# Product-key routing of an expert layer: unnormed stream transposed, the norm's factor moved into the gates, single fp32 query products, and the later heads' routing tied step by step behind the dot products

## The chip, the cores and the metric

The kernel runs on one core of one Trainium2 chip. The metric is the device time in microseconds (us) of one launch. TensorE is called PE here, VectorE DVE, ScalarE ACT, GpSimd POOL, and SyncE SP, which only starts transfers.

## The reference

Two transformer blocks run one after the other on 256 tokens of width 1024. The change touches the second half of the first block, a feed-forward layer with product keys (8 heads, 16384 experts), in float32:

```python
h = h + peer_ffn(rms_norm(h, norm_ffn), peer_w_query, peer_sub_keys, peer_down, peer_up)

q = (xf @ w_query).reshape(T, 8, 2, 128)
s = einsum('thcd,hckd->thck', q, sub_keys)            # two tables of 128 keys per head
top_s, top_i = top_k(s, 16)                           # best 16 of each table
cand_s = top_s[:, :, 0, :, None] + top_s[:, :, 1, None, :]
cand_i = top_i[..., 0, :, None] * 128 + top_i[..., 1, None, :]
best_s, pos = top_k(cand_s, 16)                       # best 16 sums: 16 experts per head and token
gates = softmax(best_s)
# per token, over its 128 chosen experts e:
a = gelu(dot(x, expert_down[e]))                      # exact gelu
out = sum(gate_e * a_e * expert_up[e])
```

`rms_norm(x, g)` is x times 1/sqrt(mean(x^2) + 1e-6), one factor for each token, times the gain g for each column.

## The kernel before

`emit` runs the phases in order. Phase A (`phase_a`) is the first block's mixer; its last step adds the output projection into the stream `x` (L589, two tiles of 128 tokens `tt`, two halves of 512 columns). Phase B (`phase_b`) is the layer above. Phases C and later are the second block.

At the start of phase B, `rms_norm` (L233 to L244) turns the sums of squares into one factor r for each token (POOL's pow, L240) and writes `xn` = x r on DVE (L244). `transpose_split` transposes `xn` on PE (L254) into `XH`, the rounded part (ACT, L258), and `XL`, the rest (DVE, L263). POOL multiplies `xn` by the gain row into `xg` (L716), which the dot products use.

`peer_route` is one head's routing, a Python generator that yields after each step. It loads 1 MB of query weights (`qraw`, L613, four buffers, SP's queue), and makes the query product `q` as three products of rounded parts: `part` splits each 512 columns of weights into `hi` (ACT, L291) and `lo` (DVE, L295), and PE runs hi XH, lo XH and hi XL (L306 to L308, for the first head L332 to L338): 48 matmuls of 256 columns for a head. Then come the copy `qT` (ACT, L619), four score matmuls `s` (L625), and on DVE the two rounds of top 16 (L602 to L606), index arithmetic (L653 to L675) and the expert numbers `idx` (L678). The gates take an Exp on ACT (L682).

The main loop has 128 rounds k (8 heads of 16 experts). In each, `fetch` gathers one row of 8 KB (down and up weights together) for each of 256 tokens: two indirect transfers of 1 MB, issued by POOL (L728) into one of ten buffers `gb`, four rounds ahead. `products` makes the two dot products on DVE (L735, `dots`) and the gelu on ACT (L737). `sums`, for the round before, multiplies by the gate (DVE, L740), makes a diagonal matrix `dg` for each token tile (ACT, L743) and adds the up rows with four fp32 matmuls of 512 columns into four PSUM tiles `u` (PE, L745). A buffer is free for the next gather when its matmuls in L745 are done. When the query weights' four buffers come free, SP loads phase C's first weights into them (`wt`, L820 and L822, four of 1 MB, the first in halves).

Head 0's routing runs to its end before the loop. Head h's is written into the rounds of head h-1, two steps in each of the first eleven rounds and the rest in the twelfth. That is only the order in which the program is written: a scheduler puts each engine's instructions in an order of its own, and each engine then runs its list in that order and waits at the front of it.

Of the kernel before, what the change touches and what calls it, by code (L numbers as in the profile page):

```python
# [9 lines left out]
F32 = mybir.dt.float32  # L10
# [175 lines left out]
class Kern:  # L186
# [25 lines left out]

    def new_xt(self, pool, tag):

        self.XH, self.XL = (pool.tile([128, 8, S], F32R, tag=tag, name=n) for n in ("XH", "XL"))

    def sp(self, name, j=0):
# [12 lines left out]
            junk = self.jk.tile([128, 512], F16, tag="junk", name="junk")  # L230
            self.last_sq = self.nc.scalar.activation(junk, xs, AF.Square, accum_out=ss)

    def rms_norm(self, sb, xn):  # L233

        nc = self.nc
        v = sb.tile([128, 2], F32, tag="rmsv", name="v")
        nc.vector.tensor_tensor(v, self.ss[:, :, 0], self.ss[:, :, 1], OP.add)
        nc.vector.tensor_scalar(v, v, 1.0 / D, 1e-6, op0=OP.mult, op1=OP.add)
        r = sb.tile([128, 2], F32, tag="rmsr", name="r")
        self.last_pow = nc.gpsimd.tensor_tensor(r, v, self.mhalf.to_broadcast([128, 2]), OP.pow)  # L240
        for h in range(2):
            c = slice(h * 512, (h + 1) * 512)
            for tt in range(2):
                nc.vector.tensor_scalar(xn[:, tt, c], self.x[:, tt, c], r[:, tt:tt + 1], None, op0=OP.mult)  # L244
# [161 lines left out]
    def phase_a(self):  # L406
        nc, tc, I = self.nc, self.tc, self.I
        with ExitStack() as es:
            sb = self.pool(es, "a_sb")
            self.spl = self.pool(es, "a_spl", bufs=4)  # L410
            wk = self.pool(es, "a_wk", bufs=2)
            ps = self.pool(es, "a_ps", bufs=4, space=PSUM)
# [5 lines left out]
            xn = sb.tile([128, 2, D], F32, tag="v", name="xn")  # L418
# [5 lines left out]
            raw, ready = self.load(I["w_qkv"][0, 0]), []  # L424
# [34 lines left out]
            t = None  # L459
            for c in range(9):  # L460
                acc = self.proj_t(ps, [I["w_qkv"][c, j] for j in range(2)], XH, XL,
                                  eng=(nc.gpsimd,) if c == 0 else None)
# [8 lines left out]
                t = wk.tile([128, 2, 512], F32, tag="qk", name="qk")  # L471
# [102 lines left out]
            for j in range(4):  # L574
# [6 lines left out]
                t = wk.tile([128, 2, S], F32, tag="cs", name="t")  # L581
# [3 lines left out]
            for n in range(2):  # L585
                acc = self.proj_t(ps, [I["w_out"][n, j] for j in range(2)], mH, mL)
                for tt in range(2):
                    xs = self.x[:, tt, n * 512:(n + 1) * 512]
                    nc.vector.tensor_add(xs, acc[tt], xs)  # L589
                    self.squares(tt, n, True if tt * n else None)  # L590
            self.hold(ps, 16)


    def norm_in(self, sb, ps, gain):
        xn = sb.tile([128, 2, D], F32, tag="xn", name="xn")
        self.rms_norm(sb, xn)
        self.transpose_split(ps, xn, gain)

    def top16(self, sb, src, n, vals, idx, work):

# [4 lines left out]
        nc.vector.max(vals[:, 8:16], work)  # L605
        nc.vector.max_index(idx[:, 8:16], vals[:, 8:16], work)  # L606

    def peer_route(self, sb, psQ, sk, io, h, idx, gates):

        nc, I = self.nc, self.I  # L610
        keep = self.tc.keep_in_program_order
        raw = self.raw.tile([128, 2048], F32, tag="raw", name="qraw")
        nc.sync.dma_start(raw.rearrange("p (a n) -> p a n", a=2), I["w_qry"][h].rearrange("a p n -> p a n"))  # L613
        acc = psQ.tile([128, 2, S], F32, tag="q", name="q")
        for n in range(2):
            self.w_tile(acc[:, n], raw, n, self.XH, self.XL, late=h == 0)
            yield
        qT = sb.tile([128, 2, S], F32, tag="qT", name="qT", bufs=2)
        nc.scalar.copy(qT, acc)  # L619
# [31 lines left out]
        p, m, q, r, t = (n32(x) for x in ("bpf", "bpm", "bpq", "bpr", "bpt"))  # L651
# [14 lines left out]
        ii = [sb.tile([128, 2, 16], F32, tag=f"i{j}", name=f"i{j}", bufs=2) for j in range(2)]  # L666
# [8 lines left out]
            nc.vector.tensor_tensor(ii[j].rearrange("p t k -> p (t k)"), u[:, :, 0], u[:, :, 1], OP.add)  # L675
            yield

        nc.vector.scalar_tensor_tensor(idx.rearrange("p k t -> p t k"), ii[0], 128.0, ii[1], op0=OP.mult, op1=OP.add)  # L678
        g = gates.rearrange("p k t -> p t k")
        e = sb.tile([128, 2, 16], F32, tag="e", name="e", bufs=2)  # L680
        nc.vector.tensor_sub(e, bs, bs[:, :, 0:1].to_broadcast([128, 2, 16]))
        nc.scalar.activation(e, e, AF.Exp)  # L682
        sm = sb.tile([128, 2], F32, tag="sm", name="sm", bufs=2)
        nc.vector.tensor_reduce(sm, e, AX.X, OP.add)
        nc.vector.reciprocal(sm, sm)
# [2 lines left out]
    def phase_b(self):  # L688

        nc, tc, I = self.nc, self.tc, self.I  # L690
        NB, AHEAD = 10, 4
        with ExitStack() as es:
            sm = self.pool(es, "b_sm")
            sb = self.pool(es, "b_q")
            self.spl = self.pool(es, "b_spl", bufs=4)
            dgp = self.pool(es, "b_dg", bufs=4)
            idx = [sm.tile([128, 16, 2], I32, name=f"idx{h}") for h in range(8)]
            gates = [sm.tile([128, 16, 2], F32, name=f"gate{h}") for h in range(8)]
            dots = sm.tile([128, 128, 2], F32, name="dots")
            act = sm.tile([128, 128, 2], F32, name="act")  # L700
            xg = sm.tile([128, 2, D], F32, name="xg")
            junk = sm.tile([128, D], mybir.dt.bfloat16, name="bjunk")
            io = sm.tile([128, 16], F16, name="io")
            nc.vector.tensor_copy(io, self.con[:, 268:284])
            sk = sm.tile([128, 16, 128], F32, name="sk")
            nc.scalar.dma_start(sk, I["sub_keys"])
            with ExitStack() as px:
                nb = self.pool(px, "b_n")
                grow = nb.tile([128, D], F32, name="grow")
                r = I["rows"]  # L710
                nc.scalar.dma_start(grow, bass.AP(tensor=r.tensor, offset=r.offset + 10 * D, ap=[[0, 128], [1, D]]))
                xn = nb.tile([128, 2, D], F32, name="xn")
                self.rms_norm(sb, xn)
                self.transpose_split(self.pool(px, "b_px", bufs=4, space=PSUM), xn, "norm_ffn")
                for tt in range(2):
                    nc.gpsimd.tensor_tensor(xg[:, tt], xn[:, tt], grow, OP.mult)  # L716
            psQ = self.pool(es, "b_psQ", bufs=2, space=PSUM)
            psU = self.pool(es, "b_psU", space=PSUM)
            gbp = self.pool(es, "b_gb", bufs=NB)
            acc = [[psU.tile([128, 512], F32, name=f"u{tt}{nh}") for nh in range(2)] for tt in range(2)]  # L720
            bufs, route = {}, [self.peer_route(sb, psQ, sk, io, h, idx[h], gates[h]) for h in range(8)]

            def fetch(k):

                bufs[k] = []
                for tt in range(2):
                    t = gbp.tile([128, 2 * D], F32, tag="gb", name="gb")
                    nc.gpsimd.indirect_dma_start(  # L728
                        t[:], None, I["experts"],
                        bass.IndirectOffsetOnAxis(ap=idx[k // 16][:, k % 16, tt:tt + 1], axis=0))  # L730
                    bufs[k].append(t)

            def products(k):
                for tt in range(2):
                    nc.vector.tensor_tensor_reduce(junk, bufs[k][tt][:, 0:D], xg[:, tt], 1.0, 0.0, OP.mult, OP.add,  # L735
                                                   dots[:, k, tt:tt + 1])
                nc.scalar.activation(act[:, k], dots[:, k], AF.Gelu)  # L737

            def sums(k):
                nc.vector.tensor_tensor(act[:, k], act[:, k], gates[k // 16][:, k % 16], OP.mult)  # L740
                for tt in range(2):
                    dg = dgp.tile([128, 128], F32, tag="dg", name="dg")
                    nc.scalar.activation(dg, self.ident, AF.Copy, scale=act[:, k, tt:tt + 1])  # L743
                    for nh in range(2):
                        nc.tensor.matmul(acc[tt][nh], dg, bufs[k][tt][:, D + nh * 512:D + nh * 512 + 512],  # L745
                                         start=k == 0, stop=k == 127)
                del bufs[k]

            for _ in route[0]:
                pass  # L750
            for k in range(AHEAD):
                fetch(k)
            for k in range(128):
                h = k // 16 + 1
                if k % 16 < 12 and h < 8:
                    for _ in range(2 if k % 16 < 11 else 99):
                        next(route[h], None)
                if k == 2:
                    self.early(sb, psQ, "s")
                if k + AHEAD < 128:  # L760
# [927 lines left out]
```

## Time and profile before

| | |
|---|---|
| median of 3 runs | 1803.95 us (1802.13 to 1807.22) |
| profiled execution | 1801.75 us, span 1800.0 us |
| PE, DVE, ACT, POOL busy | 1567.0, 943.6, 567.0, 372.4 us |
| gathers (software queue) | 268.45 MB in 36864 packets |
| first gather issued | 361.10 us |
| last dot product starts | 1033.85 us |

Times below are from the span's start. Phase A ends near 325 us, phase B near 1040 us. An engine's busy share over the whole span mixes stages with different limits, so the stages are read apart: by the 40 slices of the page, by windows, and by the timeline of one engine. A line number is one of the kernel before. A matmul in fp32 shows as two records.

### The profile page before, as it was taken

The numbers are of one execution on the slowest core, as the hardware profiler recorded it, in microseconds if no ns is written. First come the engines' busy times: TensorE is split into PE (matmuls) and PEld (weight loads), VectorE is DVE, ScalarE is ACT, GpSimd is POOL, SyncE is SP. The second block draws the span as 40 slices with busy tenths as digits, with TensorE's granted clock in tenths as the row PEclk, the third lists the DMA queues.
The fourth block names the chain that finished last, engine by engine and source line by source line (L and its number), as shares of the span: only waits on it lengthen the run. The fifth ranks groups of instructions, "written<-read, shape, count | busy, mean of one in ns | idle before, by whom it ended". The sixth has DMA issues, their size and how long they took to land. (4 is left out here: it accounts for less than half of the span.)

```text
span 1800.0 us, 21295 instructions
## 1 busy us (share of the span) xinstructions
PE 1567.0 (87%) x7436; PEld 950.1 (53%) x7436; DVE 943.6 (52%) x2376; ACT 567.0 (31%) x1296; POOL 372.4 (21%) x338
## 2 busy tenths in 40 slices
PE   9999999788887777777777798889999898899997
PEld 7889999754432223222223286653433587733442
DVE  6657756789985555555555559741111338611112
ACT  5655555433321111111111163431112356411110
POOL 3000000144353334333334202210000262100000
PEclk9999999989999999999999999999999999999999
DMA  6452445399999999999999883368999944589994
GB/s 239 174 178 103 141 165 211 133 381 367 392 393 421 421 421 421 422 421 421 422 421 422 367 339 116 136 230 350 421 416 421 414 163 167 220 341 422 421 421 182
DMA packets 88536, 568.50 MB, mean 316 GB/s; under 512 B 9265, under 2 KB 11105, under 8 KB 26465
## 3 DMA queue, kind: packets, MB, share of 16 engines
q1 hardware_dynamic: 49552, 293.85, 41.9%
q0 software_dynamic: 36864, 268.45, 36.2%
q10 hardware_dynamic: 2000, 4.70, 0.7%
q8 instruction: 63, 1.03, 0.2%
q14 instruction: 57, 0.46, 0.1%
HBM read 565.91 MB, written 1.06 MB: 315 GB/s over the span
## 5 line engine op out<-in xcount | busy, mean ns | idle before, releaser
L745 PE MATMUL u<-gb,dg 128*128 128x512 f32 x1024 | 481.9, 616 | 151.5 <-ACT dg L743 150.7
L735 DVE CUSTOM_DVE_ANT_0 bjunk<-gb,xg 128x1024 bf16<-128x1024 f32 x256 | 313.1, 1223 | 219.1 <-DMA gb<-in_experts,idx 217.9
L745 PEld LDWEIGHTS u<-gb,dg 128*128 128x128 f32 x1024 | 188.6, 193 | 436.1 <-ACT dg L743 242.0
L728 POOL DMA_INDIRECT gb<-in_experts,idx x256 | 264.4, 1033 | 414.6 <-PE u L745 320.7
L1266 PE MATMUL gu<-wt,XE 128*64 128x512 f32 x1024 | 227.7, 598 | 5.3 <-PEq L1355 5.3
L295 DVE TENSOR_TENSOR lo<-raw,hi 128x512 fp32r<-128x512 f32 x186 | 127.6, 694 | 87.5 <-ACT hi L291 86.4
L737 ACT ACTIVATE act<-dots 128x2 f32<-128x2 f32 x128 | 26.0, 203 | 442.7 <-DVE dots L735 442.7
L291 ACT CAST hi<-raw 128x512 fp32r<-128x512 f32 x192 | 117.6, 621 | 110.5 <-PE accw L307 58.4
L1266 PEld LDWEIGHTS gu<-wt,XE 128*64 128x64 f32 x1024 | 72.8, 138 | 146.9 <-issue 140.3
L1277 DVE TENSOR_TENSOR wk<-gu,wk 128x512 f32<-128x512 f32 x16 | 11.1, 692 | 242.7 <-PE gu L1266 242.7
L1320 PE MATMUL yy<-wt,wk 128*64 128x512 f32 x512 | 113.6, 595 | 11.6 <-ACT wk L1313 11.6
L894 POOL TENSOR_TENSOR lnr<-lnv,mhalf 128x2 f32<-128x2 f32 x5 | 3.5, 700 | 540.0 <-DVE lnv L893 540.0
L743 ACT ACTIVATE dg<-con,act 128x128 f32<-128x128 f32 x256 | 88.9, 394 | 47.1 <-DVE act L740 45.4
L306 PE MATMUL accw<-XH,hi 128*128 128x256 f32 x320 | 90.5, 283 | 0.0
L1327 DVE SCALAR_TENSOR_TENSOR wk<-yy,gsl,wk 128x512 fp32r<-128x512 f32 x32 | 24.0, 750 | 126.6 <-ACT wk L1326 124.9
L307 PE MATMUL accw<-XL,hi 128*128 128x256 f32 x320 | 89.1, 278 | 0.0
L308 PE MATMUL accw<-XH,lo 128*128 128x256 f32 x320 | 88.9, 278 | 0.0
L1320 PEld LDWEIGHTS yy<-wt,wk 128*64 128x64 f32 x512 | 35.3, 137 | 79.5 <-issue 62.5
L1008 DVE SCALAR_TENSOR_TENSOR y<-gl,wd,y 128x256 f32<-128x256 f32 x120 | 66.1, 551 | 4.3
L240 POOL TENSOR_TENSOR r<-v,mhalf 128x2 f32<-128x2 f32 x3 | 2.1, 709 | 306.6 <-ACT hi L291 303.0
L306 PEld LDWEIGHTS accw<-XH,hi 128*128 128x128 f32 x320 | 60.1, 188 | 1.0 <-issue 0.5
L291 ACT CAST ring<-wt 128x512 fp32r<-128x512 f32 x78 | 47.6, 620 | 40.7 <-PE acc L308 23.6
(400 smaller groups left out, 2678.7 us busy)
## 6 DMA issues: line engine op xcount, KB each, us to landing
wt<-in_m_gate SPq DMA_DIRECT2D x64, 1024.0 KB, 14.7
wt<-in_m_up SPq DMA_DIRECT2D x64, 1024.0 KB, 14.3
wt<-in_m_down SPq DMA_DIRECT2D x62, 1024.0 KB, 14.6
raw<-in_w_qkv SPq DMA_DIRECT2D x18, 1024.0 KB, 4.8
wt<-in_w_pw SPq DMA_DIRECT2D x11, 1024.0 KB, 15.9
raw<-in_w_cx SPq DMA_DIRECT2D x8, 1024.0 KB, 5.0
raw<-in_w_gc SPq DMA_DIRECT2D x8, 1024.0 KB, 4.9
qraw<-in_w_qry SPq DMA_DIRECT2D x8, 1024.0 KB, 5.3
```

The source lines that it names most:

```text
L291: copy = self.nc.scalar.copy(hi, src)
L295: (eng or self.nc.vector).tensor_tensor(lo, src, hi.bitcast(F32), OP.subtract)
L306: mm(ps, sh, mh, start=start, stop=False)
L307: mm(ps, sh, ml, start=False, stop=False)
L308: mm(ps, sl, mh, start=False, stop=stop)
L728: nc.gpsimd.indirect_dma_start(t[:], None, I["experts"], bass.IndirectOffsetOnAxis(ap=idx[k // 16][:, k % 16, tt:tt + 1], axis=0))
L735: nc.vector.tensor_tensor_reduce(junk, bufs[k][tt][:, 0:D], xg[:, tt], 1.0, 0.0, OP.mult, OP.add, dots[:, k, tt:tt + 1])
L743: nc.scalar.activation(dg, self.ident, AF.Copy, scale=act[:, k, tt:tt + 1])
L745: nc.tensor.matmul(acc[tt][nh], dg, bufs[k][tt][:, D + nh * 512:D + nh * 512 + 512], start=k == 0, stop=k == 127)
L1008: keep(nc.vector.scalar_tensor_tensor(y[:, j], gl[:, j, i:i + S], wd[:, 4 * i + j:4 * i + j + 1], y[:, j], op0=OP.mult, op1=OP.add))
L1266: nc.tensor.matmul(acc[64 * e:64 * e + 64], XE[:, k, c0 + 64 * e:c0 + 64 * e + 64], wt[:, at:at + 512], start=k == 0, stop=k == 7)
L1320: nc.tensor.matmul(yy[nh][64 * e:64 * e + 64], hT[:, f, 64 * e:64 * e + 64], wt[:, at:at + 512], start=f == 0, stop=f == 3)
```

## The change

Phase A now ends with the transposes of the stream itself: PE transposes `x`, and ACT and DVE write `XT`, fp32, times the gain, with no r. The query product of a head is one fp32 product of 16 matmuls of 256 columns, straight from the loaded weights; no part is split. The factor r reaches the result in two other places: in the scale of the Exp (now one for each token tile) and in `xg`, which ACT and POOL make after head 0's routing in the program. The keys `sk` take the second buffer of the transposed stream. The rows of the later heads' steps get `issue_after(last[0])`: every DVE instruction of a step is put behind the last dot product that the program has written so far. Steps are two a round for four rounds, then one.

```diff
@@ class Kern, end of phase_a
-            self.hold(ps, 16)
+            self.XT = self.xtp.tile([128, 8, S], F32, tag="xt", name="XTb")
+            for kp, p in self.transposes(ps):
+                for k in (2 * kp, 2 * kp + 1):
+                    if kp % 2:
+                        nc.vector.tensor_scalar(self.XT[:, k], p[:, k % 2], self.sp("norm_ffn", k), None, op0=OP.mult)
+                    else:
+                        nc.scalar.activation(self.XT[:, k], p[:, k % 2], AF.Copy, scale=self.sp("norm_ffn", k))
@@ peer_route
         for n in range(2):
-            self.w_tile(acc[:, n], raw, n, self.XH, self.XL, late=h == 0)
+            for k in range(8):
+                nc.tensor.matmul(acc[:, n], raw[:, (8 * n + k) * 128:(8 * n + k + 1) * 128], self.XT[:, k],
+                                 start=k == 0, stop=k == 7)
             yield
...
-        nc.scalar.activation(e, e, AF.Exp)
+        for tt in range(2):
+            nc.scalar.activation(e[:, tt], e[:, tt], AF.Exp, scale=rs[:, tt:tt + 1])
@@ phase_b
-            sk = sm.tile([128, 16, 128], F32, name="sk")
+            sk = self.xtp.tile([128, 16, 128], F32, tag="xt", name="sk")
...
-                self.rms_norm(sb, xn)
-                self.transpose_split(self.pool(px, "b_px", bufs=4, space=PSUM), xn, "norm_ffn")
-                for tt in range(2):
-                    nc.gpsimd.tensor_tensor(xg[:, tt], xn[:, tt], grow, OP.mult)
+            rs = self.rms_scale(sm)
...
             for _ in route[0]:
                 pass
+            last = [self.last_route.ins]
+            for tt in range(2):
+                nc.scalar.activation(xg[:, tt], self.x[:, tt], AF.Copy, scale=rs[:, tt:tt + 1])
+                nc.gpsimd.tensor_tensor(xg[:, tt], xg[:, tt], grow, OP.mult)
...
                 if k % 16 < 12 and h < 8:
-                    for _ in range(2 if k % 16 < 11 else 99):
-                        next(route[h], None)
+                    with tc.issue_after(last[0]):
+                        for _ in range(2 if k % 16 < 4 else 1 if k % 16 < 11 else 99):
+                            next(route[h], None)
```

`rms_scale` is the first part of `rms_norm`, up to r. `last[0]` is set in `products` to the round's second dot product.

On DVE, between the last add into the stream and the first search for a maximum, the list before reads (`junk`, `ss`: sums of squares; `v`: input of the pow):

```order
L589 TENSOR_TENSOR x<-acc,x 128x512 x2
L704 CAST io<-con 128x16
L228 ISA junk_3606,ss<-x 128x512
L228 ISA ss 128x1
L237 TENSOR_TENSOR v<-ss 128x2
L238 TENSOR_SCALAR v<-v 128x2
L244 TENSOR_SCALAR xn<-x,r 128x512 x4
L295 TENSOR_TENSOR lo<-qraw,hi 128x512
L263 SCALAR_TENSOR_TENSOR XL<-pt,small,XH 128x256 x8
L295 TENSOR_TENSOR lo<-qraw,hi 128x512 x7
L602 MAX tv<-s 128x8
```

and now, on the same engine at the same place:

```order
L596 TENSOR_TENSOR x<-acc,x 128x512 x2
L715 CAST io<-con 128x16
L229 ISA junk_3606,ss<-x 128x512
L229 ISA ss 128x1
L603 TENSOR_SCALAR XTb<-pt,small 128x256 x4
L238 TENSOR_TENSOR v<-ss 128x2
L239 TENSOR_SCALAR v<-v 128x2
L611 MAX tv<-s 128x8
```

The wait for r, the eight XL and the splits are gone from this place; four of the eight writes of XT stand there.

On DVE near the end of head 0's routing, the list before has head 1's searches (L602 to L606 on `tv`) and a split between head 0's last index steps:

```order
L674 TENSOR_TENSOR eq<-eq 128x32x2
L605 MAX tv<-w 128x8
L675 TENSOR_TENSOR i_3874<-eq 128x32
L674 TENSOR_TENSOR eq<-eq 128x32x4
L606 MAX_INDEX ti<-tv,w 128x8
L674 TENSOR_TENSOR eq<-eq 128x32x2
L602 MAX tv<-s 128x8
L675 TENSOR_TENSOR i_3875<-eq 128x32
L295 TENSOR_TENSOR lo<-qraw,hi 128x512
L678 SCALAR_TENSOR_TENSOR idx_3642<-i_3874,i_3875 128x2x16
```

Now head 0's steps stand alone, the dot products of round 0 follow, and head 1's first search comes behind these:

```order
L685 TENSOR_TENSOR i_3784<-eq 128x32
L698 TENSOR_TENSOR gate_3659<-e,sm 128x2x16
L684 TENSOR_TENSOR eq<-eq 128x32x2
L685 TENSOR_TENSOR i_3785<-eq 128x32
L688 SCALAR_TENSOR_TENSOR idx_3651<-i_3784,i_3785 128x2x16
L740 ISA bjunk,dots<-gb,xg 128x1024
L740 ISA dots 128x1
L740 ISA bjunk,dots<-gb,xg 128x1024
L740 ISA dots 128x1
L611 MAX tv<-s 128x8
```

On PE, from the transposes to round 1 (`u` is L745 before, L750 now; `f` is a small bias product; `s` the scores of heads 0, 1 and 2 in this order; numbers behind a name only tell buffers apart), the list now reads:

```order
L1102 MATMUL pt<-con,x 128x128 x16
L625 MATMUL q<-XTb,qraw 128x256 x18
L635 MATMUL s<-sk,qT 128x128 x4
L625 MATMUL q<-XTb,qraw 128x256 x16
L635 MATMUL s<-sk,qT 128x128 x4
L625 MATMUL q<-XTb,qraw 128x256 x37
L750 MATMUL u_3691<-gb,dg 128x512
...
L1433 MATMUL f<-t_3910,erb 8x384
L625 MATMUL q<-XTb,qraw 128x256 x2
L635 MATMUL s<-sk,qT 128x128 x4
L625 MATMUL q<-XTb,qraw 128x256 x6
L750 MATMUL u_3691<-gb,dg 128x512
```

and before, around rounds 0 and 1:

```order
L306 MATMUL q<-XH,hi 128x256
L745 MATMUL u_3733<-gb,dg 128x512
...
L1422 MATMUL f<-t_4043,erb 8x384
L745 MATMUL u_3733<-gb,dg 128x512
...
L625 MATMUL s<-sk,qT 128x128 x8
L307 MATMUL q<-XL,hi 128x256
L308 MATMUL q<-XH,lo 128x256
L306 MATMUL q<-XH,hi 128x256
```

Now 71 of the 128 query matmuls stand ahead of round 0's `u`, the other 57 between there and round 11, and head 2's scores `s` have moved ahead of round 1's `u`. Further on, three memsets and the load of the depthwise weights that phase C needs have moved from behind the loop to ahead of it.

## Rows read from the trace of the kernel before

**Rows 1.** Page, part 2: what the DMA engines moved in each of 40 slices.

```profile
GB/s 239 174 178 103 141 165 211 133 381 367 392 393 421 421 421 421 422 421 421 422 421 422 367 339 116 136 230 350 421 416 421 414 163 167 220 341 422 421 421 182
```

**Rows 2.** Windows: stretch, PE, PEld, DVE, ACT, POOL busy us, clock, DMA share, GB/s.

```profile
420.00:440.00 20.00, 16.46 (x52) 8.44 (x50) 20.00 (x89) 5.71 (x13) 7.52 (x6) 0.91 0.97 381
440.00:460.00 20.00, 19.89 (x99) 13.44 (x98) 20.00 (x81) 7.43 (x17) 9.21 (x7) 1.00 0.81 309
460.00:480.00 20.00, 19.00 (x94) 12.67 (x93) 19.96 (x95) 6.85 (x15) 7.37 (x7) 1.00 0.99 387
...
500.00:520.00 20.00, 14.65 (x29) 6.04 (x30) 18.91 (x69) 6.89 (x17) 8.86 (x7) 0.91 0.94 358
...
700.00:800.00 100.00, 74.01 (x160) 28.75 (x160) 52.50 (x100) 17.75 (x60) 37.62 (x41) 1.00 1.01 421
```

**Rows 3.** Timeline, DVE, 324 to 344 us: start us, us, line, op, count, wait.

```profile
324.94 1.39 DVE L589 TENSOR_TENSOR x<-acc,x 128x512 f32<-128x512 f32 x2 [3.56 <-PE acc L308]
...
326.37 0.69 DVE L228 CUSTOM_DVE_ANT_0 junk<-x 128x512 f16<-128x512 f32 x1
...
327.17 0.16 DVE L237 TENSOR_TENSOR v<-ss 128x2 f32<-128x2 f32 x1
327.37 0.17 DVE L238 TENSOR_SCALAR v<-v 128x2 f32<-128x2 f32 x1
...
330.91 3.23 DVE L263 SCALAR_TENSOR_TENSOR XL<-pt,small,XH 128x256 fp32r<-128x256 f32 x8
...
343.65 0.30 DVE L602 MAX8 tv<-s 128x8 f32<-128x128 f32 x1
```

**Rows 4.** Timeline, PE, 334 to 343 us: head 0's product and scores.

```profile
334.28 0.36 PE L332 MATMUL q<-XH,hi 128*128 128x256 f32 x1 [3.07 <-DVE XL L263]
...
342.45 1.16 PE L625 MATMUL s<-sk,qT 128*128 128x128 f32 x8
```

**Rows 5.** Timeline, ACT: the copy of head 0's product.

```profile
341.82 0.58 ACT L619 COPY qT<-q 128x512 f32<-128x512 f32 x1
```

**Rows 6.** Groups by shape, 1040 to 1130 us: same operations in phase C.

```profile
L852 PE MATMUL accw<-XT,wt 128*128 128x256 f32 x256 | 55.4, 379 | 0.0
...
L975 DVE TENSOR_SCALAR XT<-pt,small 128x256 f32<-128x256 f32 x4 | 1.7, 479 | 0.3 <-PE pt L971 0.3
```

**Rows 7.** Timeline, DVE, 348 to 361 us: end of head 0's routing.

```profile
348.44 0.67 DVE L295 TENSOR_TENSOR lo<-qraw,hi 128x512 fp32r<-128x512 f32 x1
...
352.13 0.28 DVE L602 MAX8 tv<-s 128x8 f32<-128x128 f32 x1
...
359.97 0.18 DVE L678 SCALAR_TENSOR_TENSOR idx<-i,i 128x32 int32<-128x32 f32 x1
```

**Rows 8.** Timeline, POOL: the product `xg` and the first gather.

```profile
331.96 5.14 POOL L716 TENSOR_TENSOR xg<-xn,grow 128x1024 f32<-128x1024 f32 x2 [3.50 <-DMA grow<-in_rows]
361.10 1.17 POOL L728 DMA_INDIRECT gb<-in_experts,idx  x1 [24.00 <-DVE tv L605]
```

**Rows 9.** Page, part 6: query weight loads, KB each, median us to landing.

```profile
qraw<-in_w_qry SPq DMA_DIRECT2D x8, 1024.0 KB, 5.3
```

**Rows 10.** Timeline, DVE: first dot of round 0, second dot of round 2.

```profile
367.07 1.23 DVE L735 CUSTOM_DVE_ANT_0 bjunk<-gb,xg 128x1024 bf16<-128x1024 f32 x1 [1.15 <-issue]
...
387.05 1.23 DVE L735 CUSTOM_DVE_ANT_0 bjunk<-gb,xg 128x1024 bf16<-128x1024 f32 x1 [0.39 <-DMA gb<-in_experts,idx]
```

**Rows 11.** Timeline, PE: eight rounds' `u` together, and two rounds late in the loop.

```profile
510.61 28.14 PE L745 MATMUL u<-gb,dg 128*128 128x512 f32 x64 [3.20 <-ACT dg L743]
...
1026.15 3.70 PE L745 MATMUL u<-gb,dg 128*128 128x512 f32 x8 [1.27 <-ACT dg L743]
1031.12 3.70 PE L745 MATMUL u<-gb,dg 128*128 128x512 f32 x8 [1.27 <-ACT dg L743]
```

**Rows 12.** Timeline, SP: last loads of phase C's weights issued in the loop.

```profile
467.67 1.97 SPq L822 DMA_DIRECT2D wt<-in_w_pw  x3
```

**Rows 13.** Windows of 4 us at the loop's start; columns as in rows 2.

```profile
368.00:372.00 4.00, 2.69 (x12) 2.69 (x13) 3.07 (x13) 0.55 (x2) 3.39 (x3) 0.50 0.98 379
```

More of the change, by code (lines that the diff above doesn't have):

```diff
@@ L213, in new_xt @@
     def new_xt(self, pool, tag):
+        self.xtp = pool
         self.XH, self.XL = (pool.tile([128, 8, S], F32R, tag=tag, name=n) for n in ("XH", "XL"))
@@ L231, in squares, with rms_scale @@
             self.last_sq = self.nc.scalar.activation(junk, xs, AF.Square, accum_out=ss)
-    def rms_norm(self, sb, xn):
+    def rms_scale(self, sb):
         nc = self.nc
@@ L240, in rms_norm @@
         self.last_pow = nc.gpsimd.tensor_tensor(r, v, self.mhalf.to_broadcast([128, 2]), OP.pow)
+        return r
+    def rms_norm(self, sb, xn):
+        nc = self.nc
+        r = self.rms_scale(sb)
         for h in range(2):
@@ L590, in phase_a @@
                     self.squares(tt, n, True if tt * n else None)
-            self.hold(ps, 16)
-    def norm_in(self, sb, ps, gain):
-        xn = sb.tile([128, 2, D], F32, tag="xn", name="xn")
-        self.rms_norm(sb, xn)
-        self.transpose_split(ps, xn, gain)
+            self.XT = self.xtp.tile([128, 8, S], F32, tag="xt", name="XTb")
[5 more added lines that the diff above has]
+                        nc.scalar.activation(self.XT[:, k], p[:, k % 2], AF.Copy, scale=self.sp("norm_ffn", k))
     def top16(self, sb, src, n, vals, idx, work):
@@ L606, in top16, with peer_route @@
         nc.vector.max_index(idx[:, 8:16], vals[:, 8:16], work)
-    def peer_route(self, sb, psQ, sk, io, h, idx, gates):
+    def peer_route(self, sb, psQ, sk, io, h, idx, gates, rs):
         nc, I = self.nc, self.I
-        keep = self.tc.keep_in_program_order
         raw = self.raw.tile([128, 2048], F32, tag="raw", name="qraw")
@@ L676, in peer_route @@
             yield
-        nc.vector.scalar_tensor_tensor(idx.rearrange("p k t -> p t k"), ii[0], 128.0, ii[1], op0=OP.mult, op1=OP.add)
+        self.last_route = nc.vector.scalar_tensor_tensor(idx.rearrange("p k t -> p t k"), ii[0], 128.0, ii[1],
+                                                         op0=OP.mult, op1=OP.add)
         g = gates.rearrange("p k t -> p t k")
@@ L694, in phase_b @@
             sb = self.pool(es, "b_q")
-            self.spl = self.pool(es, "b_spl", bufs=4)
             dgp = self.pool(es, "b_dg", bufs=4)
@@ L704, in phase_b @@
             nc.vector.tensor_copy(io, self.con[:, 268:284])
-            sk = sm.tile([128, 16, 128], F32, name="sk")
+            sk = self.xtp.tile([128, 16, 128], F32, tag="xt", name="sk")
             nc.scalar.dma_start(sk, I["sub_keys"])
[L707 to L713, printed above, removed]
-                self.transpose_split(self.pool(px, "b_px", bufs=4, space=PSUM), xn, "norm_ffn")
-                for tt in range(2):
-                    nc.gpsimd.tensor_tensor(xg[:, tt], xn[:, tt], grow, OP.mult)
+            grow = sm.tile([128, D], F32, name="grow")
+            r = I["rows"]
+            nc.scalar.dma_start(grow, bass.AP(tensor=r.tensor, offset=r.offset + 10 * D, ap=[[0, 128], [1, D]]))
+            rs = self.rms_scale(sm)
             psQ = self.pool(es, "b_psQ", bufs=2, space=PSUM)
@@ L720, in phase_b @@
             acc = [[psU.tile([128, 512], F32, name=f"u{tt}{nh}") for nh in range(2)] for tt in range(2)]
-            bufs, route = {}, [self.peer_route(sb, psQ, sk, io, h, idx[h], gates[h]) for h in range(8)]
+            bufs, route = {}, [self.peer_route(sb, psQ, sk, io, h, idx[h], gates[h], rs) for h in range(8)]
             def fetch(k):
@@ L734, in products @@
                 for tt in range(2):
-                    nc.vector.tensor_tensor_reduce(junk, bufs[k][tt][:, 0:D], xg[:, tt], 1.0, 0.0, OP.mult, OP.add,
-                                                   dots[:, k, tt:tt + 1])
+                    last[0] = nc.vector.tensor_tensor_reduce(junk, bufs[k][tt][:, 0:D], xg[:, tt], 1.0, 0.0, OP.mult,
+                                                             OP.add, dots[:, k, tt:tt + 1]).ins
                 nc.scalar.activation(act[:, k], dots[:, k], AF.Gelu)
```

## The prediction

> **What bounds the kernel now.** I read the page's slices first. From slice 12 to slice 21 (540 to 990 us) the DMA engines move 421 to 422 GB/s, always [rows 1]: this is the main loop, and nothing on an engine can shorten it. Just ahead, slices 8 to 11 show 367 to 393, and slice 7 shows 133. So I look in two places. The windows of 20 us give the first: while DVE is busy 18.91 to 20.00 of 20, the DMA rate falls to 381, 309, 387 and 358 [rows 2]. DVE is the bound there, because the list before pulls the later heads' routing and splits into the first rounds; the dot products come late, and with them the matmuls that free the buffers. In DMA time this lost 20 - 20 x rate / 421 in each window: 1.9 + 5.3 + 1.6 + 3.0 = 11.8 us. The second place is the stretch without gathers, from the last add into x (it ends at 324.94 + 1.39 = 326.33) to the first gather at 361.10 [rows 3, 8]. Its timeline is a chain: norm, xn, transposes, XL until about 334.1, first query matmul after a wait of 3.07 on XL, copy of q, scores, first MAX at 343.65, routing, idx at 359.97 [rows 3 to 5, 7]. Nothing stands beside it that the DMA could do instead, so each us saved here moves the whole loop. What follows the loop is unchanged work, and moves with it.
>
> **The change part by part: ahead of the loop.** PE can transpose x when it is added, without r. The squares stand ahead of the XT writes on DVE (0.69); the four XT writes there cost 1.7 us together in phase C [rows 3, 6]. So XT is complete at 326.33 + 0.69 + 1.7 = 328.7. The product of head 0 is 16 fp32 matmuls; 128 of that shape took 55.4 us in phase C (two records each), so 0.433 each and 6.9 in all [rows 6]: done 335.7. The copy takes 0.58, two matmuls of head 1 stand ahead of the scores, these take 1.16 [rows 4, 5]: first MAX at about 337.8 against 343.65, that is **-5.9 us**. This rests on the keys `sk` being there by 336.6. Their load now waits until XH's buffer gets its new owner, and is issued near 328.5; with the time of a query load of the same size, 5.3 [rows 9], it lands near 334. If it takes 10, the gain falls by 2 to 2.5. The other transfers and ACT's and POOL's new work on xg stand beside the routing: POOL's product, 5.14 for both tiles [rows 8], has over 15 us before the gather.
>
> From the first MAX to the end of idx head 0 took 16.5 us (343.65 to 360.15). In it stood three splits of 0.67 and eleven instructions of head 1, 0.17 to 0.30 each, some 2.65 together [rows 3, 7]: 4.65 us that go. Part of these filled gaps in which head 0's next step waited for its last one. A dependent pair of small instructions starts 0.20 apart [rows 3]; between nothing and nine such gaps come back, 0 to 1.9 us, and I take 1.65, near the full figure, as this chain is all dependent steps. That leaves **-3.0** (bounds -4.7 and -2.7). The first gather would start near 352.3: -8.9 in all, with bounds -6 and -10.5.
>
> **In the loop.** DVE loses eight splits a head, 0.67 each [rows 7], and is left with at most some 2.65 us of routing a round beside two dots of 1.23 [rows 10]: about what the DMA needs for a round, 1031.12 - 1026.15 = 4.97 [rows 11]. DVE's bound ends, and the 11.8 us are free to return. What is late next is PE. Let G be the first gather. The 71 query matmuls ahead of round 0's u cost 30.7 us from 328.7 on and are over near G + 9, before the first dots (G + 6 before [rows 8, 10]): they cost nothing. But head 2's scores now stand ahead of round 1's u, and they write where head 1's fourth search reads. That search is tied behind the dots of round 2, which ended at 388.28 = G + 27.2 and waited for the DMA there [rows 10]; they come no sooner now. Search 1, scores 1.2, six query matmuls 2.6 and u of 3.6 put the end of round 1's u at G + 36. Until then the DMA has work for rounds 0 to 5, whose buffers need no later u than round 0's: about 2 to start, 6 x 4.97 = 29.8, and one or two query loads of 1 MB, 2.5 each at 421 GB/s, so to about G + 36. After the release a gather needs about 6 us from issue to its first dot (361.10 to 367.07), of which 2.5 are the transfer itself [rows 8, 10]: idle 3.5 to 7, I take 5.5.
>
> Rounds 2 to 11 then carry the remaining 49 query matmuls, 21.2, ten u at 28.14 / 8 = 3.5 to 3.7, and 1.2 of scores: 58.4 on PE [rows 6, 11]. The gathers need 49.7, and the loads of phase C's weights, which waited for the splits until 467.67 [rows 12], now come as heads 4 to 6 free their buffers: three of 2.5, so 57.2. PE adds 1.2 more. From round 12 PE needs 3.7 of 4.97 and the DMA is the bound. So the loop loses about 6.7 where it lost 11.8: **-5.1**. Bounds: no loss at all, -11.8; or the weight loads don't fall into these rounds and the first idle stretch is 9, a loss of 8.7 + 9 = 17.7, which is +5.9.
>
> **The rest.** The memsets and the depthwise load that moved ahead of the loop stand beside it on engines with idle time: 0. The splits that ACT and PE lose are off any chain after round 0. Exp in two parts instead of one is two small ACT instructions on the gates, which are wanted rounds later (for head 0 some us later, behind the first dots): 0.
>
> Sum: -8.9 - 5.1 = -14.0 on the profiled execution's 1801.75 gives 1787.8. The median of the runs, 1803.95, lies 2.2 above that execution, so the forecast is **1790**.
>
> **Rivals.** (1) PE's late u costs nothing: the idle stretch is covered as query loads and slow first transfers keep the DMA full. For it: in 700 to 800 the rate is 421 although each u comes after a wait of 1.27 [rows 2, 11], so the gathers bear some lateness of u, how much the rows don't say. Then -8.9 - 11.8 = -20.7: 1783. (2) PE's backlog costs as much as DVE's did, or more, up to the bound of 17.7, and the way ahead of the loop gives only 6 to 9: between -9 + 6 and -6, so 1798 to 1804, taken as 1801. For it: 440 to 460, where PE was busy 19.89 of 20 and the rate lowest, 309 [rows 2]. Against: DVE was at 20.00 there as well, and PE's list is now shorter by a half of its query time. (3) Slower: TensorE's clock falls in the first rounds. In each, PE waits for the tied search or for a late dg between pieces of work; at 1.2 GHz a round's 3.6 + 2.1 of matmuls costs 5.7 more. Two and a half such rounds take all of the gain, five cost 28.5 - 14 = +14.5: 1818. For it: in 368 to 372, after PE had waited for gathers, the granted clock was 0.50 [rows 13], the lower level. Against: with PE at 19.89 of 20 it was 1.00, and in 700 to 800, where PE waits 1.27 in every round, it stayed 1.00 [rows 2, 11]. The Trainium skill (TensorE: Matmul & The Clock Gate, section "HAM oscillation — how this bites in real kernels") says that a loop whose groups of matmuls are parted by waits for transfers can start each group at the low clock; by that rule rounds 0 to 4 would all be slow, and the time this rival's. For waits as short as those of rows 11 the trace does not agree: the clock stayed 1.00. (4) The stretch ahead of the loop doesn't shorten: sk or another wait takes XL's place and the routing stays at 16 us. Then only the loop's 5.1 is left: 1799.
>
> **How the numbers follow.** The forecast (1784 to 1797) gets 0.51; rival 1 0.21, rival 2 0.13, rival 3 0.09, rival 4 0.06. A measurement of this kernel tells from no change about 0.3%, 5.4 us: faster is under 1798.5, slower over 1809.4. Faster takes the forecast, rival 1 and a third of rivals 2 and 4: 0.51 + 0.21 + 0.06 = 0.78. Same takes the other two thirds, 0.13, and 0.01 of rival 3 (two or three slow rounds): 0.14. Slower is the rest of rival 3, 0.08. The range of 1779 to 1801 leaves out rival 3, the upper half of rival 2, and little below rival 1.
>
> **What would show it.** In the changed kernel's profile: XT complete near 328.7 and the first query matmul there; first MAX near 338; idx near 351 and the first gather near 352; a dip of the DMA rate about 36 us behind the first gather, with PE waiting in front of head 2's scores; PE full and DVE well under 20 of 20 until about 95 us behind it; 421 GB/s from there on, and the last dot near 1020. It is wrong ahead of the loop if the scores wait for sk or head 0's steps still take 16 us; in the loop if DVE stays the bound, if the dip is missing or far longer, or if the granted clock of the first rounds is 0.5.

## The result and the profile after

The changed kernel takes 1786.23 us (median of 4 runs, 1784.69 to 1787.24) against 1804.03 of the kernel before; the ratio is 0.9898 (95% interval 0.9879 to 0.9916). The forecast was 1790, with 1784 to 1797 as its own range. The profiled execution takes 1785.69, which is 16.06 less than the one before; its span is 1783.9, where it was 1800.0. Three instants part these 16.1 of the span: the first gather, the last dot and the end.

| | before | after | difference | forecast |
|---|---|---|---|---|
| first gather issued | 361.10 | 352.31 | -8.79 | -8.9 |
| first gather to last dot | 672.75 | 665.99 | -6.76 | -5.1 |
| last dot to the end | 766.15 | 765.60 | -0.55 | 0 |

Phase A ended 0.46 later in this execution, so the stretch ahead of the loop is 9.25 shorter, counted from the last add into x.

Timeline of the changed kernel, DVE, which answers to [rows 3, 7, 10]:

```profile
325.40 1.40 DVE L596 TENSOR_TENSOR x<-acc,x 128x512 f32<-128x512 f32 x2 [3.56 <-PE acc L315]
...
327.46 1.66 DVE L603 TENSOR_SCALAR XTb<-pt,small 128x256 f32<-128x256 f32 x4
...
338.50 0.30 DVE L611 MAX8 tv<-s 128x8 f32<-128x128 f32 x1 [9.12 <-PE s L635]
...
351.82 0.19 DVE L688 SCALAR_TENSOR_TENSOR idx<-i,i 128x32 int32<-128x32 f32 x1
...
1018.30 1.23 DVE L740 CUSTOM_DVE_ANT_0 bjunk<-gb,xg 128x1024 bf16<-128x1024 f32 x1 [1.24 <-DMA gb<-in_experts,idx]
```

PE and POOL of the same stretch, for [rows 4, 8]:

```profile
329.37 8.01 PE L625 MATMUL q<-XTb,qraw 128*128 128x256 f32 x36 [1.53 <-DVE v L238]
337.23 1.16 PE L635 MATMUL s<-sk,qT 128*128 128x128 f32 x8
```
```profile
331.57 4.67 POOL L759 TENSOR_TENSOR xg<-xg,grow 128x1024 f32<-128x1024 f32 x2 [1.26 <-ACT xg L758]
352.31 1.17 POOL L733 DMA_INDIRECT gb<-in_experts,idx  x1 [16.07 <-DVE idx L688]
```

The first query matmul starts at 329.37, directly behind XT, and 36 records (18 matmuls) take 8.01. From first MAX to the end of idx it is 352.01 - 338.50 = 13.51, where it was 16.5. The gather waits for idx alone, and is issued 0.30 behind its end, where it was 361.10 - 360.15 = 0.95.

Windows of the changed kernel, columns as in [rows 2]:

```profile
360.00:380.00 20.00, 16.50 (x52) 9.54 (x51) 13.27 (x50) 5.60 (x10) 8.02 (x7) 0.83 1.02 422
380.00:400.00 20.00, 20.00 (x71) 12.60 (x70) 17.62 (x60) 4.69 (x15) 9.65 (x8) 1.00 1.01 420
400.00:420.00 20.00, 20.00 (x69) 12.92 (x68) 13.68 (x33) 6.85 (x18) 7.42 (x6) 1.00 1.01 422
420.00:440.00 20.00, 20.00 (x58) 10.83 (x57) 9.23 (x18) 4.10 (x13) 10.37 (x9) 1.00 1.00 380
440.00:460.00 20.00, 15.99 (x33) 6.49 (x32) 7.89 (x20) 2.19 (x7) 9.58 (x9) 0.92 1.02 419
```

Now PE is the engine at 20.00 of 20, from 380 to 440, and DVE never is. One dip is left, 380 GB/s at 420 to 440: 2.0 us of DMA time by the forecast's formula, against 11.8 before.

### The profile page after: what moved, and what is told of

The parts are those of the page before. It is cut to its first block, busy times and chain, and to the rows that moved or that the text cites. A ratio compares the mean times of both kernels' runs of the same rounds, so it can differ in the third digit from the quotient of the medians.

```text
span 1783.9 us, 20849 instructions
## 1 busy us (share of the span) xinstructions
PE 1574.6 (88%) x7276; PEld 948.6 (53%) x7276; DVE 935.0 (52%) x2336; ACT 556.7 (31%) x1274; POOL 379.9 (21%) x338
## 5 line engine op out<-in xcount | busy, mean ns | idle before, releaser
L750 PE MATMUL u<-gb,dg 128*128 128x512 f32 x1024 | 490.7, 627 | 142.2 <-ACT dg L748 141.8
L750 PEld LDWEIGHTS u<-gb,dg 128*128 128x128 f32 x1024 | 193.8, 197 | 429.3 <-ACT dg L748 227.5
L733 POOL DMA_INDIRECT gb<-in_experts,idx x256 | 272.6, 1065 | 391.8 <-PE u L750 299.7
L298 ACT CAST hi<-raw 128x512 fp32r<-128x512 f32 x192 | 117.5, 621 | 110.6 <-PE accw L314 58.4
L1288 DVE TENSOR_TENSOR wk<-gu,wk 128x512 f32<-128x512 f32 x16 | 11.1, 691 | 242.1 <-PE gu L1277 242.1
```

The costliest lines, as they stand in the source:

```text
L298: copy = self.nc.scalar.copy(hi, src)
L733: nc.gpsimd.indirect_dma_start(t[:], None, I["experts"], bass.IndirectOffsetOnAxis(ap=idx[k // 16][:, k % 16, tt:tt + 1], axis=0))
```

## The experiments

Each was timed beside the kernel before on its chip. The three lengths are those of its profiled execution: start of the adds into x to first gather, first gather to last dot, last dot to the end of the span. The diffs show only the lines that matter.

| run | median us | ratio to before (95%) | to gather | loop | rest |
|---|---|---|---|---|---|
| before | 1804.03 | 1 | 36.16 | 672.75 | 766.15 |
| after | 1786.23 | 0.9898 (0.9879 to 0.9916) | 26.91 | 665.99 | 765.60 |
| e1_no_tie | 1794.20 | 0.9952 (0.9937 to 0.9968) | 27.62 | 671.31 | 765.76 |
| e2_tie_only | 1794.94 | 0.9956 (0.9943 to 0.9969) | 34.34 | 668.00 | 768.22 |
| e3_normed | 1790.06 | 0.9929 (0.9911 to 0.9947) | 31.12 | 664.43 | 767.84 |
| e4_split3 | 1793.20 | 0.9948 (0.9931 to 0.9965) | 31.02 | 667.95 | 767.17 |
| e5_pin_pe | 1788.12 | 0.9914 (0.9894 to 0.9934) | 26.93 | 664.77 | 769.92 |
| e6_half | 1786.66 | 0.9905 (0.9888 to 0.9923) | 27.67 | 663.49 | 769.23 |
| e7_nb12 | 1786.42 | 0.9900 (0.9882 to 0.9918) | 27.57 | 663.86 | 768.71 |
| e8_both | 1785.92 | 0.9901 (0.9882 to 0.9920) | 27.66 | 664.43 | 771.74 |
| e9_two | 1785.58 | 0.9880 (0.9864 to 0.9897) | 25.24 | 665.52 | 771.94 |
| e10_two_nb12 | 1783.79 | 0.9871 (0.9855 to 0.9888) | 25.95 | 665.43 | 769.07 |
| e11_after | 1787.88 | 0.9896 (0.9880 to 0.9913) | 26.93 | 664.65 | 766.13 |

**e1_no_tie.** The changed kernel, tie undone:

```diff
-                    with tc.issue_after(last[0]):
+                    if True:
```

> The changed kernel without the tie of the later heads' steps behind the dot products; all else stays. Theory A (fp32 products take the splits from DVE, but the loop's gain needs the tie as well): seven heads of routing, some 13 us of DVE each, are pulled into the first rounds again, DVE is near 20.00 of 20 in 380 to 480 and the DMA rate falls below 400 GB/s there; head 1's searches come back between head 0's last steps, first gather 1 to 2 us later than 352.3; time 1791 (1789 to 1795). Theory B (taking the splits away is enough): no window of the loop under 400 GB/s but the one at 420 to 440, time 1785 to 1788.

Windows of this run:

```profile
380.00:400.00 20.00, 19.94 (x76) 12.87 (x75) 20.00 (x100) 8.99 (x16) 5.41 (x6) 1.00 1.02 421
400.00:420.00 20.00, 18.89 (x66) 11.29 (x65) 20.00 (x103) 6.31 (x14) 6.91 (x8) 1.00 0.99 402
420.00:440.00 20.00, 18.67 (x66) 11.40 (x65) 20.00 (x102) 6.86 (x16) 5.34 (x6) 1.00 0.95 356
440.00:460.00 20.00, 14.22 (x34) 5.95 (x32) 20.00 (x103) 5.77 (x13) 6.89 (x8) 0.91 1.01 409
460.00:480.00 20.00, 12.60 (x24) 4.96 (x24) 19.96 (x102) 5.66 (x13) 6.00 (x7) 0.91 0.94 377
480.00:500.00 20.00, 14.52 (x30) 6.35 (x31) 18.81 (x69) 7.23 (x18) 6.92 (x7) 0.91 0.86 310
```

Without the splits, but without the tie, DVE is full again and the dips lose 0.9 + 3.1 + 0.6 + 2.1 + 5.3 = 12.0 us, as many as before. The loop is 671.31, 1.4 shorter than before and 5.3 longer than after. Theory A holds: taking the splits away doesn't heal the loop. The first gather is only 0.7 later, less than expected: head 1's searches cost little at the end of head 0's routing.

**e2_tie_only.** The kernel before, and only the tie and the spread (`last` is set as in the change):

```diff
-                    for _ in range(2 if k % 16 < 11 else 99):
-                        next(route[h], None)
+                    with tc.issue_after(last[0]):
+                        for _ in range(2 if k % 16 < 4 else 1 if k % 16 < 11 else 99):
+                            next(route[h], None)
```

> The kernel before with nothing but the tie and the spread of steps (two a round for four rounds, then one); normed stream, split products and all other parts as before. Theory A (the tie is what heals the loop): first gather at about 358 (head 1's searches and splits leave head 0's end, 3 us), DVE below 18 of 20 in every window of the loop, no DMA dip as deep as 309 GB/s, loop some 7 shorter; time 1794 (1791 to 1797). Theory B (the splits are the loop's bound, wherever they are put): the first gather moves 3, the loop does not; time 1800 to 1802.

Windows of this run where [rows 2] had 309 and 387:

```profile
440.00:460.00 20.00, 19.21 (x82) 11.60 (x81) 11.89 (x27) 5.35 (x14) 6.67 (x6) 0.94 1.01 420
460.00:480.00 20.00, 16.32 (x39) 6.78 (x37) 19.30 (x78) 3.59 (x12) 9.51 (x9) 1.00 1.02 422
```

None of the dips of [rows 2] is left, with all the splits on DVE: it has time for them once they come behind the dots. One new dip stands later, 393 GB/s at 620 to 640, 1.3 us. One term was missed: DVE does reach 18.82 (at 380 to 400) and 19.30, and both windows still move 420 GB/s or more. The loop is 4.75 shorter, not 7. The tied splits hold the query loads' buffers longer, so that 276.17 MB move between first gather and last dot where it was 275.10: 2.5 us at 421 GB/s. The first gather came 1.8 earlier and not 3: head 0's routing took 13.52, the full 3.0 less, but its first MAX came 1.15 later, counted from the adds. PE's granted clock was 0.50, the lower of its two levels, from 333.3 to 340.1, in the kernel before only from 335.0 to 338.4; in both this is head 0's query product, behind a wait of 3.1 for XL.

**e3_normed.** The factor r back ahead of the transposes (Exp without scale, xg from xn; the 16 matmuls of `hold` on a constant, which end phase A in the kernel before, come back with it):

```diff
-            for kp, p in self.transposes(ps):          # end of phase_a, of x
+                self.rms_norm(sb, xn)                  # phase_b, then transposes of xn into XTb
```

> The changed kernel with the norm's factor back ahead of the transposes: xn = x r on DVE, transposes of xn, fp32 products, xg from xn on POOL, Exp without scale. Theory A: sums, pow and four products xn stand ahead of the transposes again, first query matmul near 332.4 instead of 329.37, all behind it 3 us later, loop unchanged; time 1789 (1788 to 1791). Theory B (the wait was hidden behind the transposes and writes in any case): first query matmul under 330.5, time 1786 to 1787.5.

The first query matmul of this run on PE:

```profile
333.13 8.01 PE L618 MATMUL q<-XTb,qraw 128*128 128x256 f32 x36 [1.17 <-DVE XTb L726]
```

It starts 7.52 behind the start of the adds, where the changed kernel needs 3.97: 3.55, and 4.2 to the first gather. The other 0.65 lies between the end of idx and the gather's issue, 0.96 here and 0.30 in the changed kernel. Theory A, with a price a little over the expected 3.

**e4_split3.** Split products from the unnormed stream (XH and XL written at the end of phase A):

```diff
-            for k in range(8):
-                nc.tensor.matmul(acc[:, n], raw[:, ...], self.XT[:, k], start=k == 0, stop=k == 7)
+            self.w_tile(acc[:, n], raw, n, self.XH, self.XL, late=h == 0)
```

> The changed kernel with the query products as three products of rounded parts again, from the unnormed stream; norm's factor in the gates and tie stay. Theory A: the product of head 0 itself takes as long as the fp32 one (7.5 against 7.2 us), but eight XL and splits stand on DVE ahead of it, first gather 2.5 to 3.5 later; the loop is no worse, since the splits are tied too; time 1789 (1787 to 1791). Theory B (the fp32 product carries the gain): DVE at 20 of 20 in the first 100 us of the loop, DMA dips come back, time 1795 to 1799.

The first gather comes 4.1 later than in the changed kernel, not 2.5 to 3.5: the first MAX 3.5, and 0.64 more between idx and the gather. PE of this run:

```profile
331.23 0.55 PE L339 MATMUL q<-XH,hi 128*128 128x256 f32 x1 [3.63 <-ACT hi L298]
...
334.18 0.41 PE L339 MATMUL q<-XH,hi 128*128 128x256 f32 x1
334.39 0.41 PE L340 MATMUL q<-XH,lo 128*128 128x256 f32 x1
...
337.16 0.28 PE L340 MATMUL q<-XH,lo 128*128 128x256 f32 x1
337.28 0.28 PE L339 MATMUL q<-XH,hi 128*128 128x256 f32 x1
```

Counted from the adds, the product starts 2.1 later than in the changed kernel. Behind the wait of 3.63 the granted clock was 0.50, from 330.1 to 336.9: a matmul every 0.21 us, and every 0.12 from then on. The 48 take 8.4 (331.23 to 339.65), where the 16 fp32 ones take 7.1 at 1.00. By the second half (24 in 2.9), 48 at 1.00 would take about 5.8, an estimate. So what the split product costs on this chain is the later start and the lower clock behind the wait, and not its matmuls; the expectation had neither the clock nor the step behind idx.

The loop is 667.95, as in e2, with the same 276.17 MB. So theory A holds in kind, and the loop's price, 2 us, was missed: the fp32 product also lets PE take the weights early and free their buffers ahead of the gathers.

**e5_pin_pe and e7_nb12** ask what the last dip costs.

```diff
+                        if h > 3 and lastu:
+                            pin.enter_context(tc.issue_after(lastu[0]))   # e5; lastu: last matmul of u
-        NB, AHEAD = 10, 4
+        NB, AHEAD = 12, 5                                                 # e7
```

> The changed kernel, with the query products and scores of heads 4 to 7 also tied on PE, behind the last matmul of u that the program has written so far; nothing on DVE differs. Theory A (the one dip that is left in the loop, 380 GB/s at 420 to 440, is PE working off the 57 query matmuls that stand among rounds 1 to 11): PE is under 20.00 of 20 from 380 to 440, that dip goes, loop 2 to 3 shorter, first gather unchanged at 352.3; time 1783.5 (1782 to 1785). Theory B (the dip comes from the gathers' own start, all ten buffers asked for at once): dip stays, time 1786.

> The changed kernel with twelve gather buffers in place of ten and gathers five rounds ahead. Theory A (PE's late u holds buffers back in rounds 8 to 11): a round more of buffers, 4.97 us, covers PE's lateness, the dip at 420 to 440 goes although PE stays at 20.00 of 20; loop 2 shorter, time 1784 (1783 to 1785.5). Theory B (as for the gathers' start): 24 MB-transfers at once land later each, first dots later, time 1786 to 1788.

The window of the dip, in e5:

```profile
420.00:440.00 20.00, 14.30 (x32) 5.56 (x31) 10.51 (x20) 3.58 (x12) 7.43 (x9) 1.00 1.01 421
```

and in e7:

```profile
420.00:440.00 20.00, 20.00 (x57) 10.65 (x57) 10.39 (x19) 4.32 (x13) 9.83 (x10) 1.00 1.01 420
```

In both the dip is gone, in the two ways expected. But neither time is better than that of the changed kernel, whose second timing (e11) had 412 in this window and a loop of 664.65: the dip varies by itself, and the loops of e5 and e7 lie within 0.8 of it. That PE's backlog makes the dip is shown; that it costs the loop 2 us is not.

**e6_half, e8_both, e9_two, e10_two_nb12** shorten the chain ahead of the gathers: head 0's product and scores in halves.

```diff
+            nc.scalar.copy(qT[:, 0], acc[:, 0])      # behind 11 of 16 matmuls; then two scores,
+                    done = scores(0, tt)             # five matmuls, second copy, two scores
+        s = [psQ.tile(...) for _ in range(1 if h else 2)]   # e9, e10: a tile for each table
```

> The changed kernel with head 0's product in halves: the first table's half is copied after its eight matmuls and scored before the second half's last five, and DVE searches it first. Theory A (every us of the chain ahead of the first gather moves the whole loop): first MAX near 334 instead of 338.50, wait of about 1 for the second table, first gather near 350 (2.5 earlier); time 1783.7 (1782.5 to 1785.5). Theory B (DVE's searches, in order, wait for the second table's scores so long that the start is not better): first gather within 0.7 of 352.3, time 1785.5 to 1786.5.

> The changed kernel with head 0's product in halves and with the products of heads 4 to 7 tied on PE. Theory A: both gains add, as one lies ahead of the first gather and the other behind it: first gather near 350, no window of the loop under 415 GB/s; time 1781 (1779.5 to 1783). Theory B (only one of them is on the path): 1783 to 1784.

In e6 the scores of the first table are done by 334.97, but the first MAX starts at 338.55: it waits for the scores of the second too, which lie in the same tile.

```profile
334.36 0.61 PE L637 MATMUL s<-sk,qT 128*128 128x128 f32 x4
...
337.83 0.61 PE L637 MATMUL s<-sk,qT 128*128 128x128 f32 x4
```
```profile
338.55 0.30 DVE L611 MAX8 tv<-s 128x8 f32<-128x128 f32 x1 [9.86 <-PE s L637]
```

So the chain did not get shorter, as theory B had it, but for another cause: the tile. e8, which adds e5's edit to this one, has no dip either and a loop of 664.43, within 0.3 of e11's; its time is no better. With a tile for each table the first MAX of e9 starts at 335.07:

> Head 0's product in halves as in the run before, but with the scores of the two tables in two PSUM tiles, so that the first search needs only its own table's matmuls. Theory A (the halves gave nothing because the first search waited for all four scores of the one tile): first MAX about 3 us earlier than in the changed kernel, counted from the last add into x (10 instead of 13.1), first gather 2 to 2.5 earlier, last dot 2 to 2.5 earlier; the time 1784 (1782.5 to 1786), less if the second block gives some back. Theory B (DVE's searches of the second table wait as long as before): first gather within 0.7 of the changed kernel's, time 1786.

```profile
335.07 0.30 DVE L611 MAX8 tv<-s 128x8 f32<-128x128 f32 x1 [6.39 <-PE s L637]
```

> The same with twelve gather buffers, gathers five rounds ahead. Theory A: the loop's 2 us (seen with twelve buffers alone) add to it: last dot at 1012 to 1014, time 1781.5 to 1784.5. Theory B (what is gained ahead of phase C is given back there, as PE's clock falls in its waits): last dot as early, but the time within 1 of the changed kernel's.

> The changed kernel once more, as the measure for the two others on the same chip: 1786 (1784.5 to 1788), first gather 26.9 behind the last add into x, first gather to last dot 666.

In e9 the first MAX comes 2.7 earlier than in e11, counted from the adds, as theory A had it. But routing takes 14.57 where it took 13.53, so the first gather comes only 1.7 earlier, less than the 2 to 2.5 expected, and the last dot only 0.7 (1015.46 against 1016.17). e10 has the lowest median of all, 1783.79, on the chip where the changed kernel took 1787.88; but their ratios' intervals overlap, and its profiled execution isn't shorter than e11's. I don't call it faster. Its last dot is at 1016.03, not at the 1012 to 1014 expected: the two edits don't add.

Behind the loop the profiled execution of e10 is 2.9 longer than that of e11. Granted clock (the number before the last two) in a window of phase C, e11 and then e10:

```profile
1125.00:1145.00 20.00, 15.37 (x105) 11.85 (x98) 12.26 (x18) 13.23 (x26) 6.75 (x6) 0.83 0.21 69
```
```profile
1125.00:1145.00 20.00, 15.36 (x104) 11.69 (x103) 12.43 (x18) 12.18 (x25) 6.60 (x5) 0.74 0.24 86
```

Phase C's first matmuls start as early in e10 (`accw` at 1027.4 against 1027.5), but its first expert matmul `gu` stands at 1184.1 against 1181.1. The lower clock stands beside these 3 us; that it makes them isn't shown, nor that the edit does. e11's profiled execution is the shortest of its four (1784.06 to 1788.74), e10's the longest of its four (1783.27 to 1786.93), so the difference can be that of two executions.

## Why the prediction was right, point by point

**Ahead of the loop: right, term by term.** XT, product, copy and scores: 5.9 forecast; counted from the adds, first MAX moved from 18.71 to 13.10, which is 5.6. Head 0's routing: 3.0 forecast, 3.0 measured (16.5 to 13.51). The keys `sk` were issued at 327.45 and took 6.3 to land, before the scores at 337.23; that wait did not decide. Rival 4 is out. The remaining 0.65 of the 9.25 lie between idx and the gather's issue (0.95 before, 0.30 after), a step that the forecast took as fixed. The parts depend on each other: taken out of the changed kernel one at a time, r costs 4.2 (e3), the fp32 product 4.1 (e4) and the tie 0.7 (e1), but the tie put alone into the kernel before gives 1.8 (e2). And 0.65 of e3's and e4's price is the step behind idx, which e7, another only in its gather buffers, has as well (0.94); to the first MAX each is worth 3.5. For the routing I named three splits and eleven instructions of head 1; e1, with the second but not the first, took 14.24 (338.10 to 352.34), so the splits were the larger part. The tie alone takes both away: 13.52 in e2.

**DVE as the loop's bound: right, but the cure was named by halves.** The forecast let both the splits' end and the tie relieve DVE. e1 and e2 part them: the tie alone takes the dips away, the splits' end alone doesn't. The forecast also counted eight splits a head at 0.67. There are four:

```profile
L295 DVE TENSOR_TENSOR lo<-qraw,hi 128x512 fp32r<-128x512 f32 x32 | 23.8, 752 | 2.7 <-ACT hi L291 2.7
```

(groups by shape, before, 330 to 1040 us): 32 in all, 0.75 each.

**PE as what is late next: right in kind, wrong in place.** The step that failed is "head 2's scores now stand ahead of round 1's u, and they write where head 1's fourth search reads". PE and DVE of the changed kernel:

```profile
365.74 6.44 PE L750 MATMUL u<-gb,dg 128*128 128x512 f32 x8 [3.50 <-ACT dg L748]
...
373.82 1.05 PE L635 MATMUL s<-sk,qT 128*128 128x128 f32 x8
...
377.30 3.60 PE L750 MATMUL u<-gb,dg 128*128 128x512 f32 x8
380.73 1.05 PE L635 MATMUL s<-sk,qT 128*128 128x128 f32 x8
```
```profile
378.97 0.29 DVE L611 MAX8 tv<-s 128x8 f32<-128x128 f32 x1
```

Head 2's scores ran at 373.82, with head 1's fourth search still to come at 378.97: they wait for nothing there. Head 3's, at 380.73, came just behind that search, and PE lost no time there. Round 1's u ended at 380.90, G + 28.6 instead of G + 36, and the idle stretch of 5.5 does not exist: the rate is 422 and 420 in its windows. Nor did phase C's weights come in these rounds:

```profile
433.95 0.89 SPq L831 DMA_DIRECT2D wt<-in_w_pw  x2
```

They were issued when the last query product was over. So the cover of 7.5 us by which PE would add 1.2 was not there; yet PE's 56.5 us for rounds 2 to 11 (forecast 58.4) made a dip of only 2.0: the gathers in flight covered the rest, as e7 bears out, where one more round of them took the dip away with PE as full as here. That is rival 1's mechanism, and its time, 1783, is as near as the forecast's. So it is partly luck that the loop's -5.1 lies near the measured -6.76: of the 6.7 that the forecast had as lost, the 5.5 did not come, the 1.2 came as 2.0, and a loss at the end of the loop, which it had at nothing, came in their place.

**Why not all 11.8 came back.** This the forecast had no term for. In the first 178.9 us behind the first gather the rate is 413 GB/s against 386: 11.5 us of transfer. But the last 18.3 us of the loop, in forty equal slices, before and then after:

```profile
GB/s 448 376 484 358 501 358 466 394 466 358 448 376 483 358 484 376 412 448 394 466 376 484 358 501 358 448 340 340 269 269 107 54 36 54 18 18 36 18 18 0
```
```profile
GB/s 412 430 412 394 448 412 448 394 466 394 466 376 483 358 448 412 412 430 412 376 125 161 72 90 18 36 18 36 18 36 18 36 18 36 18 18 36 18 18 0
```

Before, the transfers thin out some 4.5 us ahead of the last dot; after, 9 us ahead of it. For the last 7 us they move 18 or 36 GB/s, about one sixteenth of 421 (26). The trace's record of each packet says more: until about 1009 some 16 packets of 8 KB are on the way at once, but from 1011.3 to 1017.7 one at a time, 0.31 us each, the next starting as the one before ends. Before, this lasts only from 1031.1 to 1033.3. So one of the 16 engines is behind the others, and the last gathers wait for its share. 3.6 us of the gain are lost there: in this stretch 4.21 MB move against 5.74. With 1.1 for the 397 GB/s at 900 to 920, 11.5 - 3.6 - 1.1 = 6.8 is left, and 6.76 was measured. e5 and e7, without the dip at 420 to 440, have the same tail (4.04 and 3.84 MB), and all loops lie between 663.5 and 668.0 wherever the tie is in. This suggests that a dip in the mean rate costs only what it takes from the engine that ends last; no run tests it. Which engine that is, and why it is behind, the rows don't tell.

**The clock.** Rival 3's mechanism came for one round at the loop's start: u of round 0 took 6.44 instead of 3.60, after a wait of 3.50 on `dg`, with 0.83 in the window. It cost nothing that the DMA rate shows (422). From 380 to 440 PE had work without a gap, and the clock was 1.00. Behind that it fell in single rounds, and once beside a loss, the 1.1 us counted above:

```profile
900.00:920.00 20.00, 16.98 (x32) 6.96 (x32) 10.96 (x23) 6.44 (x18) 9.87 (x9) 0.83 0.99 397
```

There PE waited 3.38 for `dg`, the next three rounds of u took 13.27 where three take 11.1 at the 3.70 of [rows 11], and a gather waited 5.65 for its buffer. In e11 the clock of this window was 1.00, the rate 421. The Trainium skill (TensorE: Matmul & The Clock Gate, "HAM oscillation — how this bites in real kernels") tells of loops that go cold again in each wait for transfers between groups of matmuls. This loop did so only in some rounds: the clock was 0.92 in 440 to 460, where PE waited 3.63 in one round, and 1.00 in 940 to 960, where it waited 1.26 or 1.27 in each. Ahead of the loop the clock had a share that the forecast did not name: before, head 0's product ran at 0.50 from 335.0 to 338.4, behind the wait of 3.07 [rows 4]; in the changed kernel PE waited 1.53, and the clock stayed 1.00.

## What to carry to other kernels

Where a scheduler pulls ready work ahead of work that frees buffers, tie it behind that work before making it cheaper: the tie alone healed the stretch, the cheaper work alone did not. Ahead of a stretch bound by transfers most of each us of the chain counts: against e11, and counted from the adds, e3's 4.2 at the first gather were 4.0 at the last dot, e9's 1.7 were 0.8, and two executions of the changed kernel differ by 1.3 there. So a factor that can be applied later, and a product that needs no prepared operand, are worth their time on that chain, and they can spare it the lower clock that PE showed behind a wait of 3 us and more (before, e2, e4). A dip in the mean transfer rate is not yet lost time: look at the drain at the end for an engine that lags.

## What the runs showed of the hardware that was not expected

- The end of the loop waits for a lagging DMA engine: 18 to 36 GB/s for some 7 us in the changed kernel, and some 5 to 8 us of it in all ten experiments with the tie.
- One fp32 product of 16 matmuls took about 7.1 (8.01 for 18). The 48 matmuls of the three rounded products took 7.3 before (334.28 to 341.57) and 8.4 in e4, in both with a first part at a granted clock of 0.50. At 1.00, 24 of them took 2.9, so that 48 would take about 5.8, an estimate. On PE alone the fp32 product is thus not the shorter one; its gain was in what PE waits for, and in the clock behind the wait.
